# A pinned order for the first chunks of a four-layer decoder trunk, with x loaded in quarters and the second constants loaded later

## The chip, the cores and the metric

The kernel runs on one core of a Trainium2 chip. The metric is device time in microseconds for one execution of the whole program, the lower the better. A profiled execution also gives a trace: the start and length of every instruction on the matrix engine (TensorE, in the rows PE, and PEld for its weight loads), VectorE (DVE), ScalarE (ACT) and GpSimd (POOL), and of the DMA issues on the queue of SyncE (SP) and of ScalarE (ACTq). Times inside an execution count from the start of its span.

## The reference

Four residual layers over x of 256 tokens by 1024 features. Layer i has a token mixer (sliding-window attention with sinks, gated linear attention, forgetting attention, then sliding-window attention again) and a SwiGLU feed-forward part. Ahead of each stands a norm, whose result is shifted and scaled by vectors computed from a conditioning vector c:

```python
c_act = jax.nn.silu(c)
for i in range(DEPTH):
    mod = c_act @ ada_w[i] + ada_b[i]
    sh1, sc1, g1, sh2, sc2, g2 = jnp.split(mod, 6, axis=-1)
    h = rmsnorm(x, norm_gain[i, 0]) * (1 + sc1) + sh1
    x = x + g1 * mixer(h)
    h = rmsnorm(x, norm_gain[i, 1]) * (1 + sc2) + sh2
    x = x + g2 * swiglu(h)
return rmsnorm(x, final_norm)
```

So the very first thing to be computed, before any product of the first mixer, is sh1 and sc1 of layer 0: c times two matrices of 1024 by 1024, which have to come from memory first.

## The kernel before

x is kept on chip feature-major: eight k blocks of 128 features by 256 tokens. Weights are float32 and are streamed once. `Stream` holds a fixed list of items (`items`, L1164), each a transfer of up to 1 MB into one of five `raw` buffers (`load_raw`, L179). An item is issued on the SP queue as soon as, in the order of the list, a buffer is free; SP waits in order, so a load whose buffer isn't free holds up those behind it. A weight item ("w") is split by ACT and DVE into a high part `wh` (a cast, L194) and a low part `wl` (a subtraction, L196), in two pieces; a product of two such split operands is three matmuls (`mm3`, L275 to 279). An "ada" item holds a piece of a matrix that c is multiplied by.

For the first two vectors of layer 0, called here s (the scale, vector 1) and h (the shift, vector 0), an item holds 256 columns, and `ada_rows` (L217) makes 16 small matmuls with c (L228), a copy of the row by ACT (L229), and then a "turn": two small products, four matmul records, that stand the row up into columns (L233), and an addition of the bias on DVE (L235). The list begins, in the letters of `ORDER0`, with s h w s h s h w s h w w w: four pairs of s and h, and between them the weights w0 and w1 of the mixer's first two chunks (`i0_0` keys, `i0_1` values); w2 is the third chunk, `i0_2`.

`first_chunks` (L712) makes the first norm's statistics (squares of the eight k blocks on ACT L422, sums on DVE L433, small matmuls L326, L339, L349, a square root L342), and then goes through four rounds r. A round takes the s and h items of two k blocks, computes their columns of mod and A (`mod_cols`, L378), makes the two k blocks of the normed and shifted input, `hh` and `hl` (`h_tiles`: tk on DVE L452, hh on ACT L454, hl on DVE L447), and multiplies them with w0, and from round 2 on also with w1. (In the rows, hh is the tile of that name; "the h row" is the shift.) The order in which this is written is not the order in which it runs: the tile scheduler sorts each engine's instructions by its own estimate, apart from those marked to keep their place.

The constants come in two transfers: `const` on the SP queue at the beginning, and `const2` (0.67 MB: rotary tables, masks, and the sinks) on ACT's queue within `first_chunks`. `swa` (L751) follows: rotary products of the keys, the products of four more chunks, and the attention. `nsink` (L690) negates the sinks on DVE.

Of the kernel before, what the change touches and what calls it, by code (L numbers as in the profile page):

```python
# [13 lines left out]
AF = mybir.ActivationFunctionType  # L14
ALU = mybir.AluOpType
PSUM = bass.MemoryType.PSUM

P = 128
D = 1024
KT = D // P  # L20
S = 256
# [11 lines left out]
CONST_COLS = [  # L33
    ("ident", 128), ("ones", 2), ("eps", 1), ("gain", DEPTH * 2 * KT), ("ada_b", DEPTH * 48),
    ("fin", KT), ("hnorm", 2), ("bgate", GH), ("bf", 1), ("one", 1), ("c", KT),
]
CONST2_COLS = [
    ("cos", NB * HD), ("sin", NB * HD), ("swamask", 3 * P), ("foxmask", 3 * P), ("scan", S),
    ("sinks", 2 * 16),
]  # L40


# [100 lines left out]
class Builder:  # L143
# [542 lines left out]
    def swa_heads(self, layer, pool, q_of, kT, v, oh, ol):  # L686
# [7 lines left out]
        def head(h):  # L694
            g, i = divmod(h, 4)
            rows = slice((i % 2) * HD, (i % 2 + 1) * HD)

            def pre():
                q = q_of(g)
                if g not in qTs and q is not None:  # L700
                    qTs[g] = self.swa_qT(pool, q)
                return q is not None
            return {
                "pre": pre, "ready": lambda: True,
                "q": lambda: qTs[g][rows, i // 2],
                "k": lambda: kT[0][rows, g],
                "v": lambda: [v[:, b, g * HD:(g + 1) * HD] for b in range(NB)],
                "sink": nsink[:, h:h + 1],
            }
        return self.attn_heads(pool, [head(h) for h in range(16)], self.c("swamask"), oh, ol)  # L710

    def first_chunks(self):  # L712

        nc = self.nc
        self.A, self.late = None, []
        self.st.cap = self.st.widx[EARLY]
        self.per_tick = 0.0
        self.turns = []
        for k in range(KT):
            self.x_done(k, nc.vector)  # L720
        self.stat_start(self.acc)
        self.stat_end()
        self.tc.keep_in_program_order(nc.scalar.dma_start(self.const2, self.a["const2"]))
        rbs = self.t(self.small, [P, S], "rbs", bufs=1)
        nc.scalar.copy(rbs, self.spread(self.y))
        hs = hh, hl = self.h_alloc()
        A = self.t(self.small, [P, KT], "A", bufs=2)
        sh = self.mod[0][:, :KT]
        outs, ws, todo = [], [], []
        for r in range(4):  # L730
            self.st.force_ada(0, (0, 1), r)
            while self.turns:
                self.turns.pop(0)()
            self.mod_cols(0, 0, 2 * r, 2 * r + 2, A)
            self.h_tiles(range(2 * r, 2 * r + 2), rbs, A, sh, hh, hl)
            if r in (0, 2):
                c = len(ws)
                ws.append([x.rearrange("p (k n) -> p k n", k=KT) for x in self.st.get(f"i0_{c}")])
                self.st.cap = self.st.widx[EARLY]
                outs.append(self.banks(("mm", "s")[c])[0])  # L740
                todo.append(0)
            for c, (wh, wl) in enumerate(ws):
                for k in range(todo[c], 2 * r + 2):
                    for m in range(2):
                        sl = slice(m * P, (m + 1) * P)
                        self.mm3(outs[c][m][:, :S], hh[:, k, sl], hl[:, k, sl], wh[:, k], wl[:, k],
                                 k == 0, k == KT - 1)
                todo[c] = 2 * r + 2
        return hs, [[o[:, :S] for o in out] for out in outs]

    def swa(self, layer, oh, ol, pool):  # L751
# [480 lines left out]
    def build(self):  # L1232
        nc, tc, ctx = self.nc, self.tc, self.ctx
        pool = lambda n: ctx.enter_context(tc.tile_pool(name=n, bufs=1))
        cp = pool("const")
        self.wpool = pool("w")
        self.hpool = pool("h")
        self.small = pool("small")
        self.psum = ctx.enter_context(tc.tile_pool(name="ps", bufs=1, space=PSUM))

        self.x = self.t(cp, [P, KT, S], "x")
        self.const = self.t(cp, [P, CONST_W], "const")
        self.const2 = self.t(cp, [P, CONST2_W], "const2")
        self.cact = self.t(cp, [P, D], "cact")
        self.mod = [self.t(cp, [P, 48], f"mod{l}") for l in range(DEPTH)]
        self.gla_wg = self.t(cp, [16, GH * P], "gla_wg")
        self.gla_masks = self.t(cp, [P, 7, P], "gla_masks", U8)

        crow = self.t(self.hpool, [P, KT, S], "hh", bufs=1).rearrange("p k n -> p (k n)")[:1, :D]
        nc.sync.dma_start(crow, self.a["c"])  # L1250
        nc.sync.dma_start(self.const, self.a["const"])
        nc.sync.dma_start(self.x, self.a["x"])
        self.ccol = self.t(self.small, [P, KT, 32], "ccol", bufs=1)
        nc.vector.memset(self.ccol, 0.0)
        nc.scalar.activation(self.ccol[:, :, 0:1], self.c("c").unsqueeze(2), AF.Silu)
        self.st = Stream(self, self.items())
        self.st.issue()
        one = self.t(self.small, [P, S], "fc", bufs=2)[:1, :P]
        nc.vector.memset(one, 1.0)
        for i in range(2):  # L1260
            ps = self.ps("t")
            sl = slice(i * 512, (i + 1) * 512)
            nc.tensor.matmul(ps, one, crow[:, sl], start=True, stop=True)
            nc.scalar.activation(self.cact[:, sl], ps, AF.Silu)

        mixers = [self.swa, self.gla, self.fox]
        for l in range(DEPTH):
            with tc.tile_pool(name=f"mix{l}", bufs=1, reuse_waits="tile") as mp:
                self.layer = l
                self.done_k = 0  # L1270
                oh = self.t(mp, [P, KT, S], "oh", F32R)
                ol = self.t(mp, [P, KT, S], "ol", F32R)
                self.cuts, self.on_pool = CUTS[0], MIX_POOL[l]
                mixers[l % 3](l, oh, ol, mp)
                self.cuts, self.on_pool = CUTS[1], OUT_POOL
                self.out_proj(l, oh, ol, self.mod[l][:, 2 * KT:3 * KT])
            self.cuts, self.on_pool = CUTS[2], FFN_POOL
            self.ffn(l)
        self.final_tile(KT - 1)
        stat = self.ps("o")  # L1280
        self.stat = [stat[:, b:b + 1] for b in range(NB)]
        self.stat_end(self.acc)
        for i, ps in enumerate(self.final):
            o = self.t(self.wpool, [P, WIDE], "raw", bufs=RAW)[:, :512]
            b, half = divmod(i, 2)
            y = self.y[:, b:b + 1]
            if b:
                nc.scalar.activation(o, ps, AF.Copy, scale=y)
            else:
                nc.vector.tensor_scalar(out=o, in0=ps, scalar1=y, scalar2=None, op0=ALU.mult)  # L1290
            (nc.scalar if b else nc.sync).dma_start(
                self.out[b * P:(b + 1) * P, half * 512:(half + 1) * 512], o)
# [108 lines left out]
```

## Time and profile before

| | before |
|---|---|
| median of 3 runs | 1260.54 us (1259.45 to 1266.03) |
| the profiled execution | 1260.51 us |
| its span | 1258.7 us |
| mean granted TensorE clock | 0.986 |
| busy: PE, DVE, ACT, POOL | 96%, 79%, 55%, 11% |
| read from memory | 296.16 MB, 236 GB/s over the span |
| issue of c, const and x on SP | 0.75, 1.15 and 1.56 us |
| first product with c | 14.50 us |
| first product of w2, behind the first chunks | 55.44 us |

A row of the timeline gives the start, the length, the engine, the line, the operation with its output and inputs, and the count of like instructions merged into it; in square brackets stands the idle time of the engine before it and what ended it. Matmul rows are pipelined: the distance between two starts says more than the length of one. The chain of waits follows the last instruction back to what released it, and gives shares of the span.

### The profile page before, as it was taken

What the parts mean: (1) busy time and instruction counts of PE and PEld (TensorE: products, weight loads), DVE (VectorE), ACT (ScalarE), POOL (GpSimd) and SP (SyncE); (2) the same over time, 40 slices, a digit from 0 to 9 for tenths busy, and PEclk for the clock granted to TensorE, in tenths of its full rate; (3) what the DMA queues carried; (4) which work ended last, traced back from release to release, by engine and by line L of the source; (5) the groups of instructions that cost most, each with busy time, mean ns of one, the idle gap of its engine ahead of it and who ended that gap; (6) DMA issues with size and microseconds to landing.
All of it is one profiled execution on the core that took longest, in us unless ns stands there. A gap on an engine that the chain in (4) does not pass through costs nothing.

```text
span 1258.7 us, 19761 instructions
## 1 busy us (share of the span) xinstructions
PE 1207.7 (96%) x7444; PEld 1053.3 (84%) x7444; DVE 1000.2 (79%) x1826; ACT 698.3 (55%) x1294; POOL 136.3 (11%) x177
## 2 busy tenths in 40 slices
PE   5898799999998999999999999999999999999997
PEld 3786788888888998888889999888888979888886
DVE  2598998888779989988878758988888998766553
ACT  3475564444486756444557867544445677544442
POOL 0011110001104412000011101100011011000011
PEclk8898899999999999999999999999999999999999
DMA  8655779977745445988875543699788444665440
GB/s 358 250 220 203 271 282 364 336 284 260 280 148 183 147 141 204 363 323 306 274 281 214 206 174 135 250 349 339 281 274 281 168 164 168 215 220 211 162 162 34
DMA packets 44673, 298.51 MB, mean 237 GB/s; under 512 B 5169, under 2 KB 5329, under 8 KB 14242
## 3 DMA queue, kind: packets, MB, share of 16 engines
q1 hardware_dynamic: 43778, 295.54, 64.9%
q8 instruction: 58, 0.95, 0.3%
q10 hardware_dynamic: 432, 1.20, 0.2%
q0 software_dynamic: 368, 0.53, 0.1%
q14 instruction: 37, 0.30, 0.1%
HBM read 296.16 MB, written 1.05 MB: 236 GB/s over the span
## 4 chain that ended last, share of the span: by engine, by line
PE 84%; DVE 7%; ACT 4%; issue 2%; DMA 2%; POOL 1%; DVEq 0%; SPq 0%; ACTq 0%; POOLq 0%
PE mm L1133 13%; PE mm L277 12%; PE mm L278 11%; PE mm L279 11%; PE s L278 7%; PE s L277 7%; PE s L279 7%; PE mm L1135 7%; PE s L576 2%; DVE wl L196 2%; PE o L606 2%; DVE raw L213 1%; PE t L1104 1%; PE t L617 1%; ACT wh L194 1%
## 5 line engine op out<-in xcount | busy, mean ns | idle before, releaser
L196 DVE TENSOR_TENSOR wl<-raw,wh 128x1024 fp32r<-128x1024 f32 (+2 forms) x408 | 447.2, 1129 | 88.0 <-ACT wh L194 86.9
L194 ACT CAST wh<-raw 128x1024 fp32r<-128x1024 f32 (+2 forms) x408 | 376.2, 964 | 230.7 <-issue 108.8
L1133 PE MATMUL mm<-a,wh 128*128 128x512 f32 x704 | 247.8, 396 | 0.0
L213 DVE CUSTOM_DVE_ANT_0 raw<-raw,cact,const 128x1024 f32<-128x1024 f32 x176 | 224.1, 1292 | 11.2 <-DMA raw<-in_ada 11.1
L277 PE MATMUL mm<-wh,hh 128*128 128x512 f32 (+1 forms) x560 | 198.8, 356 | 6.1 <-ACT hh L454 5.8
L1135 PE MATMUL mm<-a,wl 128*128 128x256 f32 x704 | 197.6, 281 | 0.0
L278 PE MATMUL mm<-wl,hh 128*128 128x512 f32 (+1 forms) x560 | 194.5, 348 | 0.2 <-DVE wl L196 0.2
L279 PE MATMUL mm<-wh,hl 128*128 128x512 f32 (+1 forms) x560 | 193.5, 347 | 0.0
L1133 PEld LDWEIGHTS mm<-a,wh 128*128 128x128 f32 x704 | 132.2, 188 | 30.4
L277 PE MATMUL s<-wh,hh 128*128 128x512 f32 (+2 forms) x384 | 145.1, 379 | 2.9 <-ACT hh L454 2.9
L278 PE MATMUL s<-wl,hh 128*128 128x512 f32 (+2 forms) x384 | 143.6, 375 | 0.6 <-DVE wl L196 0.6
L279 PE MATMUL s<-wh,hl 128*128 128x512 f32 (+2 forms) x384 | 142.1, 374 | 0.0
L433 POOL TENSOR_TENSOR sq<-sq,sq 128x256 f32<-128x256 f32 x48 | 53.9, 1123 | 758.4 <-ACT sq L422 732.2
L1135 PEld LDWEIGHTS mm<-a,wl 128*128 128x128 f32 x704 | 132.6, 188 | 0.2
L277 PEld LDWEIGHTS mm<-wh,hh 128*128 128x128 f32 x560 | 107.0, 191 | 21.3 <-ACT hh L454 6.2
L278 PEld LDWEIGHTS mm<-wl,hh 128*128 128x128 f32 x560 | 107.1, 192 | 12.8 <-issue 0.7
L279 PEld LDWEIGHTS mm<-wh,hl 128*128 128x128 f32 x560 | 106.9, 192 | 13.0 <-issue 0.2
L514 DVE SCALAR_TENSOR_TENSOR x<-mm,mod,x 128x256 f32<-128x256 f32 x128 | 61.5, 481 | 44.7 <-PE mm L1135 37.5
L277 PEld LDWEIGHTS s<-wh,hh 128*128 128x128 f32 x384 | 72.5, 189 | 15.5 <-ACT hh L454 3.4
L278 PEld LDWEIGHTS s<-wl,hh 128*128 128x128 f32 x384 | 72.8, 190 | 12.6 <-DVE wl L196 0.8
L279 PEld LDWEIGHTS s<-wh,hl 128*128 128x128 f32 x384 | 72.2, 190 | 13.1
L277 PE MATMUL mm<-oh,wh 128*128 128x256 f32 x256 | 74.8, 297 | 8.3 <-DVE x L514 8.2
(218 smaller groups left out, 2007.8 us busy)
## 6 DMA issues: line engine op xcount, KB each, us to landing
raw<-in_ada SPq DMA_DIRECT2D x96, 1024.0 KB, 6.3
raw<-in_gu SPq DMA_DIRECT2D x88, 1024.0 KB, 5.6
raw<-in_down SPq DMA_DIRECT2D x64, 704.0 KB, 4.7
raw<-in_swa_in SPq DMA_DIRECT2D x12, 1024.0 KB, 5.3
raw<-in_gla_in SPq DMA_DIRECT2D x11, 1024.0 KB, 4.9
raw<-in_fox_in SPq DMA_DIRECT2D x11, 1024.0 KB, 6.0
raw<-in_swa_o SPq DMA_DIRECT2D x8, 1024.0 KB, 5.0
raw<-in_gla_o SPq DMA_DIRECT2D x4, 1024.0 KB, 4.8
```

The lines of the kernel that those rows point to most:

```text
L194: nc.scalar.copy(wh[:, sl], raw[:, sl])
L196: eng.tensor_tensor(out=wl[:, sl], in0=raw[:, sl], in1=wh[:, sl].bitcast(F32), op=ALU.subtract)
L213: nc.vector.tensor_tensor_reduce(out=w, in0=w, in1=self.cact, scale=1.0, scalar=b, op0=ALU.mult, op1=ALU.add, accum_out=col)
L277: nc.tensor.matmul(out, ah, bh, start=first, stop=False)
L278: nc.tensor.matmul(out, ah, bl, start=False, stop=False)
L279: nc.tensor.matmul(out, al, bh, start=False, stop=last)
L433: (eng or nc.gpsimd).tensor_tensor(out=q, in0=self.acc, in1=q, op=ALU.add)
L514: self.nc.vector.scalar_tensor_tensor(out=self.x[:, m], in0=ps, scalar=gate[:, m:m + 1], in1=self.x[:, m], op0=ALU.mult, op1=ALU.add)
L576: nc.tensor.matmul(sc[:, so:s1], q[:, so:so + P], k[:, :k1], start=True, stop=True)
L606: nc.tensor.matmul(o[rows, b * P:S], vs[e][b], pt[:, e, :S] if b == 0 else pt[:, e, S:], start=b == 0, stop=b == 1)
L1133: nc.tensor.matmul(o, wh[:, k], a[:, kk].rearrange("p e n -> p (e n)"), start=kk == 0, stop=False)
L1135: nc.tensor.matmul(o[:, S:], wl[:, k], a[:, kk, 0], start=False, stop=kk == FT - 1)
```

## The change

- The sinks move from `const2` to `const`.
- x is loaded in four transfers of two k blocks, and the weight stream's first loads are issued before the other preparations.
- Silu of c is computed on the row `crow` before it is spread over the partitions; the two copies to `cact` then run on DVE instead of ACT, out of other banks of PSUM ("mm" instead of "t").
- The squares and sums of the first norm are written out in `first_chunks`.
- In a round, s's product comes first, then chunk 0's products of the round before, then h's product, then both turns and the h tiles. Chunk 1's products all come behind the rounds: first those of six k blocks, then the last two k blocks of both chunks.
- `const2` is issued on ACT's queue at the end of round 1 instead of behind the statistics.
- `pinned` chains all instructions of `first_chunks` on each engine to the order in which they are written.

```diff
 CONST_COLS = [
...
+    ("sinks", 2 * 16),
 ]
 CONST2_COLS = [
...
-    ("sinks", 2 * 16),
 ]
...
+    def pinned(self, start):
+        last = {}
+        for ins in list(self.nc.cur_bb.bb.instructions)[start:]:
+            if ins.engine in last:
+                self.tc.add_manual_dep(
+                    ins, last[ins.engine].name,
+                    mybir.DependencyInfo(mybir.DependencyClass.NoSync, mybir.DependencyReason.DATA),
+                    reason="first chunks")
+            last[ins.engine] = ins
...
     def first_chunks(self):
         nc = self.nc
+        start = len(nc.cur_bb.bb.instructions)
...
+        acc = None
         for k in range(KT):
-            self.x_done(k, nc.vector)
+            q = self.t(self.small, [P, S], "sq", bufs=4)
+            nc.scalar.activation(q, self.x[:, k], AF.Square)
+            if 0 < k < KT - 1:
+                nc.vector.tensor_tensor(out=q, in0=acc, in1=q, op=ALU.add)
+            acc, self.acc = q, acc
+        self.last_sq = acc
         self.stat_start(self.acc)
         self.stat_end()
-        self.tc.keep_in_program_order(nc.scalar.dma_start(self.const2, self.a["const2"]))
...
+        def products(n, chunks=slice(None)):
+            for c, (wh, wl) in list(enumerate(ws))[chunks]:
+                for k in range(todo[c], n):
+                    for m in range(2):
+                        sl = slice(m * P, (m + 1) * P)
+                        self.mm3(outs[c][m][:, :S], hh[:, k, sl], hl[:, k, sl], wh[:, k], wl[:, k],
+                                 k == 0, k == KT - 1)
+                todo[c] = n
         for r in range(4):
-            self.st.force_ada(0, (0, 1), r)
+            self.st.force_ada(0, (1,), r)
+            products(2 * r, slice(1))
+            self.st.force_ada(0, (0,), r)
             while self.turns:
                 self.turns.pop(0)()
             self.mod_cols(0, 0, 2 * r, 2 * r + 2, A)
...
-            for c, (wh, wl) in enumerate(ws):
-                for k in range(todo[c], 2 * r + 2):
...
-                todo[c] = 2 * r + 2
+            if r == 1:
+                nc.scalar.dma_start(self.const2, self.a["const2"])
+        products(KT - 2)
+        products(KT)
+        self.pinned(start)
...
-        nc.sync.dma_start(self.x, self.a["x"])
+        for i in range(4):
+            nc.sync.dma_start(self.x[:, 2 * i:2 * i + 2], self.a["x"][:, 2 * i:2 * i + 2])
+        self.st = Stream(self, self.items())
+        self.st.issue()
         self.ccol = self.t(self.small, [P, KT, 32], "ccol", bufs=1)
         nc.vector.memset(self.ccol, 0.0)
-        nc.scalar.activation(self.ccol[:, :, 0:1], self.c("c").unsqueeze(2), AF.Silu)
-        self.st = Stream(self, self.items())
-        self.st.issue()
         one = self.t(self.small, [P, S], "fc", bufs=2)[:1, :P]
         nc.vector.memset(one, 1.0)
+        nc.scalar.activation(crow, crow, AF.Silu)
+        nc.scalar.activation(self.ccol[:, :, 0:1], self.c("c").unsqueeze(2), AF.Silu)
         for i in range(2):
-            ps = self.ps("t")
+            ps = self.ps("mm")
             sl = slice(i * 512, (i + 1) * 512)
             nc.tensor.matmul(ps, one, crow[:, sl], start=True, stop=True)
-            nc.scalar.activation(self.cact[:, sl], ps, AF.Silu)
+            nc.vector.tensor_copy(self.cact[:, sl], ps)
```

More of the change, by code (lines that the diff above doesn't have):

```diff
@@ L741, in first_chunks @@
                 todo.append(0)
-            for c, (wh, wl) in enumerate(ws):
-                for k in range(todo[c], 2 * r + 2):
[L744 to L747, printed above, removed]
-                todo[c] = 2 * r + 2
+            if r == 1:
[3 more added lines that the diff above has]
+        self.pinned(start)
         return hs, [[o[:, :S] for o in out] for out in outs]
```

## The prediction

> **What bounds the kernel now.** I read the page first, then the begin of the chain of waits, then the timeline of the first 70 us and a table of stages cut at the rounds of `first_chunks`. The page says that the kernel as a whole is TensorE's:
>
> ```profile
> span 1258.7 us, 19761 instructions
> PE 1207.7 (96%) x7444; PEld 1053.3 (84%) x7444; DVE 1000.2 (79%) x1826; ACT 698.3 (55%) x1294; POOL 136.3 (11%) x177
> ...
> PE 84%; DVE 7%; ACT 4%; issue 2%; DMA 2%; POOL 1%; DVEq 0%; SPq 0%; ACTq 0%; POOLq 0%
> ```
>
> The profiled execution took 1260.51 us, 1.81 more than its span; the median of the runs is 1260.54, so a microsecond off the span is taken as one off the median. PE is idle for 1258.7 − 1207.7 = 51 us, and the change can only work on the part that lies in the beginning. There the stages are short and serial (columns: stretch, length, PE, PEld, DVE, ACT and POOL busy with counts, granted clock, DMA share, GB/s):
>
> ```profile
> core 0: us, PE busy (x) PEld busy (x) DVE busy (x) ACT busy (x) POOL busy (x), PEclk, DMA share, GB/s
> 14.50:22.25 7.75, 4.67 (x42) 2.43 (x41) 1.55 (x7) 2.62 (x6) 1.02 (x4) 0.94 1.01 425
> 22.25:25.67 3.42, 3.23 (x13) 2.71 (x13) 2.86 (x4) 1.28 (x2) 0.00 (x0) 0.50 0.78 328
> 25.67:31.77 6.10, 4.15 (x41) 2.06 (x40) 1.38 (x6) 1.30 (x4) 0.00 (x0) 0.78 0.92 340
> 31.77:34.63 2.86, 2.86 (x13) 2.63 (x13) 0.87 (x2) 0.35 (x1) 0.00 (x0) 0.50 0.90 335
> 34.63:39.99 5.36, 3.40 (x42) 1.91 (x41) 1.39 (x6) 1.30 (x4) 0.00 (x0) 0.97 0.61 216
> 39.99:46.86 6.87, 6.24 (x49) 5.90 (x49) 3.23 (x4) 2.23 (x3) 0.00 (x0) 1.00 0.71 247
> 46.86:50.97 4.11, 3.07 (x41) 1.97 (x40) 1.28 (x6) 1.30 (x4) 0.00 (x0) 1.00 0.73 253
> ```
>
> From 14.5 to 51 us no engine is full: rows of products with c (14.50, 25.67, 34.63, 46.86) alternate with rows of products of h, and in the former PE is idle for up to 3 us while ACT and DVE turn a row of mod into h. In two stretches the clock is 0.50 as well. This is a latency chain, so order decides, not work. The end of the stage is the first product of w2 (`i0_2`, the first ordinary chunk), at 55.44:
>
> ```profile
> 55.44 0.28 PE L277 MATMUL mm<-wh,hh 128*128 128x256 f32 x1
> ```
>
> **The start, up to the first product with c (call its time T0).** Before:
>
> ```profile
> 1.56 0.42 SPq L1252 DMA_DIRECT2D x<-in_x  x1
> 2.28 3.75 PE L1263 MATMUL t<-hh,fc 1*128 1x512 f32 x4 [2.28 <-DMA hh<-in_c]
> 3.77 1.28 ACT L1255 ACT_TABLE_LOAD   x1 [3.77 <-DMA const<-in_const]
> 6.07 0.60 ACT L1264 ACTIVATE cact<-t 128x512 f32<-128x512 f32 x1 [0.31 <-PE t L1263]
> 7.03 3.23 ACT L422 ACTIVATE sq<-x 128x256 f32<-128x256 f32 x8 [0.37 <-DMA x<-in_x]
> 7.79 3.08 DVE L433 TENSOR_TENSOR sq<-sq,sq 128x256 f32<-128x256 f32 x6 [6.52 <-ACT sq L422]
> 10.92 1.01 PE L326 MATMUL t<-const,sq 128*128 128x1 f32 x4 [4.89 <-DVE sq L433]
> 14.50 3.56 PE L228 MATMUL t<-raw,ccol 128*32 128x256 f32 x32
> 18.41 1.05 ACT L194 CAST wh<-raw 128x1024 fp32r<-128x1024 f32 x1
> ```
>
> c is there at 2.28; the table load (1.28) now waits for c alone, then Silu runs over 1024 elements of one partition (the nearest row is the cast of 1024 columns, 1.05) and over ccol: ACT is free at about 4.8 instead of 6.67. x in quarters gives the first squares their data earlier; the last quarter can't land before x did, 7.03, and three more issues of 0.42 can put it at 8.3. Eight squares at 3.23 / 8 = 0.40 then end near 8.1 to 9.1, instead of 10.26. But the two copies to cact move from ACT to DVE (the same shape took ACT 0.60), and the second waits for the matmuls, which start only behind Silu: 4.6 + 3.75 = 8.4. The six sums take 3.1 on DVE (last end before: 10.87). Best, copies and sums interleave: about 9.4. Worst, the tile scheduler puts all sums behind the second copy: 8.4 + 0.6 + 3.1 = 12.1. From the last sum to T0 it was 14.50 − 10.87 = 3.6, and nothing in that chain changes but the const2 issue on ACT, which leaves. T0 is 13.0 at best, 15.7 at worst; I take 14.4, the middle, close to the row's 14.50: **no gain here**.
>
> The transfers themselves aren't slowed, I think:
>
> ```profile
> x<-in_x SPq DMA_DIRECT2D x1, 1024.0 KB, 5.4
> const<-in_const ACTq DMA_DIRECT2D x1, 656.0 KB, 8.0
> const<-in_const SPq DMA_DIRECT2D x1, 205.5 KB, 2.5
> ```
>
> 205.5 KB took 2.5 us and 1 MB took 5.4, all of it under way together, so landing times overlap and quarters shouldn't cost four times 2.5. The Trainium skill, "DMA: Bandwidth & Descriptors", section "Measured (HBM→SBUF, 128 partitions, SWDGE, issued from GpSimd)", asks for batches of at least 1 MiB and so speaks against quarters of x. By the page's fixed 2.0 us for each, an estimate one behind the other is 10.4 us for x; the trace's overlap disagrees.
>
> **Round 0.** Before, DVE stood for const2, because the scheduler had put `nsink` (from `sinks`, which lay in const2) ahead of A:
>
> ```profile
> 17.99 1.18 PE L233 MATMUL t<-const,fc 128*128 128x1 f32 x8
> 20.83 0.18 DVE L690 TENSOR_SCALAR nsink<-const 128x16 f32<-128x16 f32 x1 [1.98 <-DMA const<-in_const]
> 21.96 1.22 DVE L196 TENSOR_TENSOR wl<-raw,wh 128x1024 fp32r<-128x1024 f32 x1
> 23.23 0.80 PE L278 MATMUL mm<-wl,hh 128*128 128x256 f32 x2 [0.19 <-DVE wl L196]
> 25.67 1.94 PE L228 MATMUL t<-raw,ccol 128*32 128x256 f32 x16
> ```
>
> 1.98 us of waiting go, since sinks now lie in const. What is late next is the split of w0. Before, its first cast ran at 18.41 under the wait; pinned, both casts stand behind the two hh on ACT. The turns end at T0 + 4.7 (19.17 − 14.50); mod, A, tk and two hh take 2.0 (worked out from round 2's rows below: 0.30 + 0.16 + 0.48 + 0.91, and the gaps), cast 1.05, wl 1.22: the second product runs at T0 + 9.0 = 23.4, as before (23.23). So that gain is spent on the order of the casts. The products, at clock 0.50, take 25.67 − 23.23 = 2.4 again: 25.8. Here the new order first pays: s1's product already ran in the gap, so only h1's is left, 1.94 at half clock: it ends at 27.7. Before, at 25.67, s1's was just starting, and h1's came behind s1's turn.
>
> **Rounds 1 to 3.** Rows of round 2 before, at full clock:
>
> ```profile
> 36.91 1.07 PE L228 MATMUL t<-raw,ccol 128*32 128x256 f32 x16
> 37.28 0.16 DVE L378 SCALAR_TENSOR_TENSOR A<-mod,const 128x2 f32<-128x2 f32 x1
> 37.48 0.88 DVE L452 SCALAR_TENSOR_TENSOR tk<-rbs,A,x 128x256 f32<-128x256 f32 x2
> 38.52 0.61 PE L233 MATMUL t<-const,fc 128*128 128x1 f32 x4 [0.55 <-ACT fc L229]
> 39.43 0.91 ACT L454 ACTIVATE hh<-tk,mod 128x256 fp32r<-128x256 f32 x2 [0.96 <-DVE mod L235]
> 39.99 0.39 PE L277 MATMUL mm<-wh,hh 128*128 128x256 f32 x1 [0.86 <-ACT hh L454]
> 41.44 0.28 PE L279 MATMUL mm<-wh,hl 128*128 128x256 f32 x1
> 43.05 0.28 PE L279 MATMUL s<-wh,hl 128*128 128x256 f32 x1
> 46.65 0.28 PE L279 MATMUL s<-wh,hl 128*128 128x256 f32 x1
> ```
>
> h's product ends at 37.98, and the first product of the new h runs at 39.99: 2.0. Both turns now stand behind h's product, so A (0.16) and the first tk (0.48), which ran under it, come on the path: 2.65. In that gap the turns end after 1.15 (39.13 − 37.98), and the next round's s product (1.07) fits into the 1.5 left. Then 12 products, 41.56 − 39.99 = 1.6, and the next h product, 1.07. A round is 2.65 + 1.6 + 1.07 = 5.3, where before round 2 began at 34.63 and round 3 at 46.86. h2's product ends at 33.0, h3's at 38.3, the last turns at 39.5. Chunk 1's six k blocks, now put off to here, are 36 matmuls of 0.12 (43.05 to 46.65 is thirty): 43.8. They hide the last hh (38.3 + 2.65 = 41.0); without them PE would stand 1.5. The last 24 take 2.9: 46.7. The sum is 55.44 − 46.7 = **8.7 us**.
>
> **What has to be there in time.** SP issues in order, and w1's load stands ahead of s3's and h3's; it waits for w0's buffer, that is for the second half of the split, T0 + 10.2 = 24.6. 1.05 MB at the 425 GB/s of the first row of stages is 2.5 us; with about 1 us to start, w1, s3 and h3 are in by 33.1, and with const2 (0.67 MB, 1.6, now issued behind round 1's hh on ACT, where the copy of s2's row is all that it holds up for 0.4) by 34.7. s3 is wanted at 34.2 and landed near 30.6; h3 is wanted at 37.2. The cover is 2.5 us; beyond it each us costs one. const2 is first read by the rotary products, behind chunk 0's end near 45: 10 us of cover. w1's casts stand behind round 2's hh, near 36; its split ends near 39.5, when chunk 1 starts, no slack.
>
> Behind this nothing hangs on absolute time: the loads follow the buffers, and DVE's queue is full from 80 to 100, so a shift is handed on.
>
> ```profile
> 80.00:100.00 20.00, 18.93 (x152) 15.82 (x150) 20.00 (x67) 14.35 (x46) 6.87 (x12) 1.00 0.60 222
> 100.00:130.00 30.00, 24.15 (x148) 18.16 (x146) 26.08 (x66) 13.32 (x42) 2.48 (x8) 0.84 0.57 199
> ```
>
> With w2's split (two wl of 1.22) now able to run in DVE's idle time, up to 2.4 more could come off that full stretch. One half-clock window would cost 3.4 x (1 − 0.12 / 0.22) = 1.5, where 0.22 is 2.86 / 13 of the row at 31.77. So the forecast is 1260.5 − 8.7 = **1251.8**, its own range 8.7 − 1.4 − 1.5 = 5.8 to 8.7 + 1.4 + 2.4 = 12.5 of gain: 1248.0 to 1254.7.
>
> **Rivals.**
> 1. *Half the beginning cold.* The clock stays at 0.50 after 27.7. Cost against the forecast: two h products 0.87 each, two s products that no longer fit their gap (0.4 each), 24 products at 0.22 instead of 0.13 (2.2), 60 at 0.22 instead of 0.12 (6.0): 10.7, so the stage ends 2.0 us later than before, **1262.5**. It is slower than before from the point at which over 8.7 / 10.7 = 81% of 27 to 47 us is at half clock. For it: 22.25 to 25.67 and 31.77 to 34.63 show 0.50. Against: both follow long gaps of PE, and in the new order PE has 3.7 of each 5.3 us at work. The whole: 0.05. A middle, half of it cold, gives 8.7 − 5.3 = 3.4, **1257.1**: 0.10. The Trainium skill, "TensorE: Matmul & The Clock Gate", section "What's actually happening", says that the array falls to half after an idle window of about 3.4 us; the stretch of 2.86 at 0.50 at 31.77 is of that size.
> 2. *x's quarters land one behind the other.* Four times 2.5 from 1.56 puts the last at 11.6; two squares, the last sum and 3.6 more make T0 16.9 to 17.0, 2.6 later than taken: a gain of 6.1, **1254.4**. The rows' overlap speaks against it: 0.05. The Trainium skill's page cited for x is the rule that would lead here.
> 3. *The pin changes little.* If the scheduler's order already was nearly this, or another wait (w0's split, w1's load) ends each round as late as before, only const2's 1.98 go: **1258.5**. Against it, the rows at 25.67 and 36.91 show s, turn, h, turn and only then the products. 0.12.
> 4. *What lies behind is sorted worse.* The pin ends with `first_chunks`, and the scheduler sorts the rest anew. From 80 to 130 PE is idle 1.07 + 5.85 = 6.9; if that grew by twice as much again, 13.8 − 8.7 = 5.1 slower, **1265.6**; it decides from 8.7 lost on. 0.06.
>
> **How the numbers follow.** Forecast 0.62, rivals 0.05 + 0.10, 0.05, 0.12, 0.06. 0.5% is 6.3 us, about what a measurement of this kernel tells from no change. Faster by more: the forecast, 0.62. Within: the cold cases, the late x and the weak pin, 0.32. Slower by more: rival 4, whose price reaches 6.3 only at its worst, counted whole, 0.06. The range runs from the best of the forecast's own, 1248.0, to past rival 3, 1259.0; outside lie the whole of rival 1, rival 4, and the tails.
>
> **What would show it.** T0 between 13 and 15.7; no DVE wait on const2; second product of round 0 near 23.4; h products ending near 27.7, 33.0 and 38.3; the clock at 1.00 from about 28; 60 matmuls in a row from 39.5; w2's first product near 46.7; and the later stages at the same lengths, each some 8.7 us earlier. I am wrong if PE waits for s3's or h3's load, if the rounds stay above 7 us, or if the lead is gone by 130 us.

## The result, and the profile after

The median of 14 runs of the changed kernel is 1254.2 us (1251.11 to 1257.54), of 14 runs of the kernel before 1264.12 (1259.45 to 1272.07). The ratio is 0.9921, with a 95% interval of 0.9906 to 0.9936: 10 us faster. The profiled execution took 1254.5 us, against 1260.51 before. So trace against trace 6.0 us are gone, and run against run 9.9. The two numbers differ because 1260.5, from which the prediction counted, lies near the lower end of what the kernel before does; its runs and their clock are taken up again at the end of "Why the prediction was right".

The page of the changed kernel, the lines that answer to those shown of before (span and count; busy time of each engine; shares of the chain of waits):

```profile
span 1252.7 us, 19770 instructions
PE 1207.5 (96%) x7444; PEld 1051.5 (84%) x7444; DVE 1001.1 (80%) x1828; ACT 697.8 (56%) x1293; POOL 133.9 (11%) x177
...
PE 85%; DVE 8%; ACT 3%; issue 2%; POOL 1%; DMA 1%; SPq 0%; DVEq 0%; ACTq 0%; POOLq 0%
```

PE is busy for the same time (1207.5 against 1207.7) and idle for 45 us instead of 51. PE's work is the same; what went is waiting. In its timeline the steps that the prediction named (`...` stands for rows left out):

```profile
0.74 1.28 ACT L1287 ACT_TABLE_LOAD   x1 [0.74 <-PEq L1419]
...
3.81 0.17 DVE L690 TENSOR_SCALAR nsink<-const 128x16 f32<-128x16 f32 x1 [2.54 <-DMA const<-in_const]
...
8.68 0.72 ACT L735 ACTIVATE sq<-x 128x256 f32<-128x256 f32 x2 [0.42 <-DMA x<-in_x]
...
10.27 1.02 PE L326 MATMUL t<-const,sq 128*128 128x1 f32 x4 [3.07 <-DVE sq L737]
...
13.84 3.64 PE L228 MATMUL t<-raw,ccol 128*32 128x256 f32 x32
...
18.66 1.07 PE L228 MATMUL t<-raw,ccol 128*32 128x256 f32 x16
...
22.77 0.58 PE L278 MATMUL mm<-wl,hh 128*128 128x256 f32 x1 [0.68 <-DVE wl L196]
...
25.42 1.94 PE L228 MATMUL t<-raw,ccol 128*32 128x256 f32 x16
...
29.08 1.93 PE L228 MATMUL t<-raw,ccol 128*32 128x256 f32 x16
...
33.81 1.66 PE L228 MATMUL t<-raw,ccol 128*32 128x256 f32 x16
...
36.56 1.07 PE L228 MATMUL t<-raw,ccol 128*32 128x256 f32 x16
...
39.98 1.07 PE L228 MATMUL t<-raw,ccol 128*32 128x256 f32 x16
...
49.34 0.28 PE L277 MATMUL mm<-wh,hh 128*128 128x256 f32 x1
```

`nsink` runs at 3.81, as soon as const is there, and holds up nothing. The last squares wait for x's last quarter and start at 8.68. The rows of L228 are, in this order, s0 with h0 (the products with the first items of s and h), s1, h1, s2, h2, s3 and h3. From s1 on each stands alone, where before, in rounds 1 and 2, s, its turn and h followed one another. The last row is w2's first product: 49.34, where it was 55.44. The same table of stages as for the kernel before, cut at this kernel's rounds (stretch, length, PE, PEld, DVE, ACT and POOL busy, clock, DMA share, GB/s):

```profile
13.84:21.51 7.67, 5.89 (x57) 3.04 (x56) 2.17 (x8) 3.01 (x7) 0.00 (x0) 0.99 1.01 427
21.51:25.42 3.91, 3.23 (x13) 2.71 (x13) 2.34 (x2) 1.17 (x2) 0.00 (x0) 0.50 0.95 358
25.42:30.95 5.53, 5.53 (x42) 2.98 (x41) 1.63 (x6) 1.27 (x3) 0.00 (x0) 0.50 0.95 388
30.95:33.81 2.86, 2.86 (x17) 2.64 (x13) 0.52 (x2) 0.38 (x2) 0.00 (x0) 0.50 0.96 369
33.81:38.08 4.27, 3.80 (x41) 2.06 (x41) 1.29 (x6) 0.93 (x3) 0.00 (x0) 0.85 0.97 391
38.08:42.06 3.98, 3.95 (x36) 2.95 (x37) 3.33 (x5) 3.39 (x6) 0.00 (x0) 1.00 0.56 232
42.06:49.34 7.28, 7.28 (x63) 7.28 (x62) 5.78 (x13) 3.52 (x6) 0.00 (x0) 1.00 0.89 348
```

Before, PE was idle in the stretches of products with c for 1.0 to 3.1 us each; here it is full from 25.42 on, but for half a microsecond in the row of 33.81. What is left to see is the clock: 0.50 from 21.5 to 33.8 and still 0.85 in the row behind. The forecast had 1.00 from 28. And the DMA engines (the wire, below) are busier: a share of 0.95 and more up to 38, where the stretch at 34.63 of the kernel before had 0.61.

A clock of 0.50 is called cold below, 1.00 warm. In the traces' records of the clock, cold stretches last 3.41 us or a multiple of it (but for the one in which a trace ends), and one such length is called a window. The changed kernel has four cold windows ahead of w2, from 21.4 to 35.1. The kernel before has four as well: three in its rounds, and one behind the last row that the prediction shows, in the last products ahead of w2. The next row of that table is:

```profile
50.97:55.44 4.47, 4.47 (x25) 4.47 (x25) 3.60 (x10) 2.62 (x5) 0.00 (x0) 0.62 0.81 326
```

So the lead of 6.1 us at w2 was reached with as much cold time as before, 13.7 us in each trace behind its first record of the clock, at about 18: between these two traces, a shorter cold time doesn't explain it.

### The profile page after: what moved, and what is told of

Same layout as the page of the kernel before. It is cut to its first block, busy times and chain, and to the rows that moved or that the text cites. A ratio compares the mean times of both kernels' runs of the same rounds, so it can differ in the third digit from the quotient of the medians.

```text
span 1252.7 us, 19770 instructions
## 1 busy us (share of the span) xinstructions
PE 1207.5 (96%) x7444; PEld 1051.5 (84%) x7444; DVE 1001.1 (80%) x1828; ACT 697.8 (56%) x1293; POOL 133.9 (11%) x177
## 4 chain that ended last, share of the span: by engine, by line
PE 85%; DVE 8%; ACT 3%; issue 2%; POOL 1%; DMA 1%; SPq 0%; DVEq 0%; ACTq 0%; POOLq 0%
PE mm L1160 13%; PE mm L277 12%; PE mm L278 12%; PE mm L279 11%; PE s L277 7%; PE s L278 7%; PE s L279 7%; PE mm L1162 7%; PE s L576 2%; DVE wl L196 2%; PE o L606 2%; DVE raw L213 2%; PE t L1131 1%; ACT wh L194 1%; PE t L617 1%
## 5 line engine op out<-in xcount | busy, mean ns | idle before, releaser
L213 DVE CUSTOM_DVE_ANT_0 raw<-raw,cact,const 128x1024 f32<-128x1024 f32 x176 | 224.2, 1292 | 16.7 <-DMA raw<-in_ada 16.5
L514 DVE SCALAR_TENSOR_TENSOR x<-mm,mod,x 128x256 f32<-128x256 f32 x128 | 61.5, 481 | 42.9 <-PE mm L1162 35.2
```

Of the source, the lines that this page charges most:

```text
L213: nc.vector.tensor_tensor_reduce(out=w, in0=w, in1=self.cact, scale=1.0, scalar=b, op0=ALU.mult, op1=ALU.add, accum_out=col)
L514: self.nc.vector.scalar_tensor_tensor(out=self.x[:, m], in0=ps, scalar=gate[:, m:m + 1], in1=self.x[:, m], op0=ALU.mult, op1=ALU.add)
```

## The experiments

Ratios are to the kernel before, with the 95% interval. "w2" is w2's first product in the profiled execution: 55.44 before, 49.34 in the changed kernel. The theory was that the new order of the rounds is the gain; the rivals were that it was const2, x, the pin as such, or the clock.

**1. The old order, pinned.** The changed kernel, but its rounds in the old order:

```diff
-            self.st.force_ada(0, (1,), r)
-            products(2 * r, slice(1))
-            self.st.force_ada(0, (0,), r)
+            self.st.force_ada(0, (0, 1), r)
...
+            products(2 * r + 2)
             if r == 1:
                 nc.scalar.dma_start(self.const2, self.a["const2"])
-        products(KT - 2)
-        products(KT)
```

> The changed kernel with one part undone: each round is written, and pinned, in the old order (s, h, both turns, h tiles, then the round's products of both chunks); the start, the sinks, x in quarters, const2 after round 1 and the pin stay. My theory (the new order of the rounds is the gain): h1's product can only start behind s1's, near 27, chunk 1's products stand ahead of s3's, and the last products end near 54: w2's first product at 53 to 57 us, within 0.3% of the kernel before (ratio 0.996 to 1.001). Rival (the pin, the constants or x pay): w2's first product near 49.3 as in the changed kernel, ratio near 0.992.

Measured: ratio 0.9976 (0.9959 to 0.9994), w2 at 56.94. Its rounds, in its timeline:

```profile
25.96 3.22 PE L228 MATMUL t<-raw,ccol 128*32 128x256 f32 x32
...
34.74 2.25 PE L228 MATMUL t<-raw,ccol 128*32 128x256 f32 x32
...
46.58 1.93 PE L228 MATMUL t<-raw,ccol 128*32 128x256 f32 x32
...
56.94 0.28 PE L277 MATMUL mm<-wh,hh 128*128 128x256 f32 x1
```

The rounds are 8.8 and 11.8 apart, where those of the kernel before were 9.0 and 12.2 (25.67, 34.63, 46.86). With the start, the constants and the pin all in place the lead is gone from the trace, and of the time 0.24% is left of 0.79%. The order is what pays most, as the theory had it. The clock doesn't explain the difference: the mean granted clock of these runs is 0.987, that of the changed kernel's 0.988.

**2. The new order, not pinned.** The line `self.pinned(start)` is left out.

> The changed kernel without the pin: the text is in the new order, but the scheduler sorts each engine by its own estimate. As it sorts it, h's turn stands apart from s's, chunk 0's products lie partly around the s product, and const2's transfer is the first instruction on ACT, ahead of x on the wire. My theory: the part of the order that the scheduler keeps pays in part, and const2 (0.66 MB at some 425 GB/s) makes x, s0 and h0 up to 1.5 us later: T0 near 15, w2's first product at 50.5 to 54, ratio 0.994 to 0.999. Rival (the pin is not needed, the new text alone does it): w2's first product within 0.7 of 49.3, ratio 0.991 to 0.993.

Measured: ratio 0.9991 (0.9970 to 1.0012), w2 at 53.70:

```profile
0.74 0.38 ACTq L772 DMA_DIRECT2D const<-in_const  x1
...
12.46 1.01 PE L326 MATMUL t<-const,sq 128*128 128x1 f32 x4 [5.05 <-DVE sq L737]
...
16.03 0.66 PE L228 MATMUL t<-raw,ccol 128*32 128x256 f32 x4
```

The scheduler makes const2's transfer ACT's first instruction, and x, const and the statistics come later: 12.46 instead of 10.27, T0 16.03. Its rounds, too, have the turns pulled apart again, and the timed gain is nil. So the text alone does nothing that can be measured: the order pays, and here the pin is what holds it. How much of the loss is the early const2 and how much the order of the rounds, this run does not separate.

**3. The sinks alone.** The kernel before with the entry `("sinks", 2 * 16)` moved from `CONST2_COLS` to `CONST_COLS`, nothing else.

> The kernel before with one part of the change alone: the sinks lie in const, so nsink on DVE does not wait for const2. PE's order is that of the kernel before. My theory: the 1.98 us of DVE's wait go, the second product of round 0 comes at 21 to 22 instead of 23.23, w2's first product 1 to 2 us earlier than 55.4: ratio 0.998 to 0.9995. Rival 3 of the prediction turned round (const2 was most of it): ratio 0.995 or less.

Measured: ratio 0.9981 (0.9964 to 0.9999), in the range expected. But its trace has w2 at 51.21, 4.2 us earlier, and not the 1 to 2 expected. The second product of round 0 (20.93) explains 2.3 of them. The rest goes with the clock, which is cold in one window of the rounds, not three. The lead is then lost. The out projection of layer 0, from the first to the ninth sum into x (L514), in this kernel, the one before and the changed one:

```profile
107.19:139.79 32.60, 24.62 (x143) 19.52 (x141) 26.32 (x57) 13.66 (x34) 0.61 (x4) 0.76 0.57 209
```
```profile
111.45:139.36 27.91, 19.68 (x139) 16.41 (x137) 26.33 (x58) 12.98 (x33) 0.61 (x4) 0.94 0.66 243
```
```profile
105.32:133.21 27.89, 18.63 (x139) 15.36 (x137) 26.31 (x57) 12.96 (x33) 0.60 (x4) 0.95 0.66 244
```

32.60 us at a mean clock of 0.76, against 27.91 at 0.94 and 27.89 at 0.95. What a beginning gains, a cold stretch later can take; it is the same work in all three. That a shift of the beginning made this stretch cold was not tested: it is one trace.

**4. x in one transfer.** The changed kernel with `nc.sync.dma_start(self.x, self.a["x"])`.

> The changed kernel with x in one transfer again; its order on PE behind that is the same. My theory: squares start near 7.0 instead of 5.49 and the last sum is 0 to 0.7 us later, T0 13.8 to 14.5, and what that costs is lost in the noise: ratio to the kernel before 0.991 to 0.994, w2's first product 49.3 to 50.2. Rival (the quarters bring the start forward, and the start counts in full): T0 15 or later, ratio 0.0015 worse than the changed kernel. Rival of the page on DMA (quarters cost): T0 earlier than 13.5.

Measured: ratio 0.9906 (0.9878 to 0.9934), not to be told from the changed kernel's. In the trace the start is later:

```profile
8.41 0.68 DVE L1292 COPY cact<-mm 128x512 f32<-128x512 f32 x1
...
10.40 0.68 DVE L1292 COPY cact<-mm 128x512 f32<-128x512 f32 x1
...
11.01 0.94 DVE L737 TENSOR_TENSOR sq<-sq,sq 128x256 f32<-128x256 f32 x2
```

The squares begin at 7.32, and both copies to cact stand ahead of the last two sums, so T0 is 15.57, 1.7 behind the changed kernel's 13.84; w2 is at 51.10, 0.9 later than the theory had it. The rival was right on T0 (15 or later), but the times don't show that it counts; the other rival, T0 earlier than 13.5, did not happen.

**5 and 6. Both kernels again**, unchanged, for second traces.

> The kernel before, unchanged, for a second trace of it. The runs of before spread from 1257 to 1272 us and the trace that the prediction used (1260.5) lies near their lower end. My theory: the beginning repeats (w2's first product at 55 to 56 us), and what differs lies between 95 and 145 us, in stretches in which the granted clock is 0.50: the first 64 sums into x then end at another time by up to 5 us. Rival: the beginning itself varies, and w2's first product comes up to 4 us later than 55.4.

> The changed kernel, unchanged, for a second trace on the chip of the next two and a ratio beside theirs. My theory: w2's first product at 46 to 50 us, depending on how many of the windows from 21 to 35 us run at clock 0.50 (the first trace: all four, 49.3); ratio 0.990 to 0.994. Rival (the four cold windows were an accident): w2's first product near the forecast 46.7.

Measured: the kernel before took 1261.65 us with w2 at 54.08; the changed kernel's ratio is 0.9925 (0.9899 to 0.9951), with w2 at 49.47.

```profile
54.08 0.28 PE L277 MATMUL mm<-wh,hh 128*128 128x256 f32 x1
```
```profile
49.47 0.28 PE L277 MATMUL mm<-wh,hh 128*128 128x256 f32 x1
```

For the kernel before, both the theory (55 to 56) and its rival (up to 4 us later) missed: w2 came 1.4 us earlier, with one cold window fewer ahead of it, three instead of four, and the later stages did not vary by the 5 us expected. For the changed kernel the theory held: w2 is in its range, and the same four windows are cold.

**7. Split and A earlier.** Round 0's first half of w0's split stands ahead of hh and hl, and A and the first tk ahead of h's part of mod:

```diff
-            while self.turns:
-                self.turns.pop(0)()
+            self.turns.pop(0)()
             self.mod_cols(0, 0, 2 * r, 2 * r + 2, A)
-            self.h_tiles(range(2 * r, 2 * r + 2), rbs, A, sh, hh, hl)
+            tks = []
+            for k in range(2 * r, 2 * r + 2):
+                tk = self.t(self.small, [P, S], "tk", bufs=3)
+                nc.vector.scalar_tensor_tensor(out=tk, in0=rbs, scalar=A[:, k:k + 1], in1=self.x[:, k],
+                                               op0=ALU.mult, op1=ALU.mult)
+                tks.append((k, tk))
+                if self.turns:
+                    self.turns.pop(0)()
+            if r == 0:
+                self.st.piece()
+            for k, tk in tks:
+                nc.scalar.activation(hh[:, k], tk, AF.Identity, bias=sh[:, k:k + 1])
+            for k, tk in tks:
+                nc.vector.scalar_tensor_tensor(out=hl[:, k], in0=tk, scalar=sh[:, k:k + 1],
+                                               in1=hh[:, k].bitcast(F32), op0=ALU.add, op1=ALU.subtract)
```

> The changed kernel with two steps of a round moved on ACT and DVE: the first half of w0's split stands ahead of round 0's hh and hl, and in all rounds A and the first tk stand ahead of h's part of mod. PE's order and all behind the first chunks stay. Theory (PE waits on that split and on A and tk): the second product of round 0 at 21.2 to 21.6 instead of 22.77, and 0.4 to 0.6 off each of four rounds: w2's first product 2.5 to 3.5 us earlier than the changed kernel's on the same clock, and ratio 0.002 to 0.003 better. Rival (the loads or the clock set the rounds, not these): w2's first product within 1 us of it.

Measured: ratio 0.9914 (0.9889 to 0.9939), w2 at 46.22.

```profile
19.88 1.61 PE L228 MATMUL t<-raw,ccol 128*32 128x256 f32 x16 [1.27 <-DMA raw<-in_ada]
...
21.80 0.42 PE L278 MATMUL mm<-wl,hh 128*128 128x256 f32 x1
...
32.73 1.07 PE L228 MATMUL t<-raw,ccol 128*32 128x256 f32 x16 [1.30 <-DMA raw<-in_ada]
...
46.22 0.28 PE L277 MATMUL mm<-wh,hh 128*128 128x256 f32 x1
```

The second product runs at 21.80 instead of 22.77, less than expected, because PE now waits for s1's load (1.27) and later for s3's (1.30): what is late next are the loads. w2 is 3.1 earlier, but on a warmer clock (two cold windows, not four), so not all of it is the split's. The time missed: 0.0007 better than the changed kernel's 0.9921, where 0.002 to 0.003 was expected, and not to be told from it.

**8. Unread products in PE's gap.** In the changed kernel, behind s1's product:

```diff
             self.st.force_ada(0, (1,), r)
+            if r == 1:
+                fill = self.ps("o")
+                for _ in range(5):
+                    nc.tensor.matmul(fill[:, :P], self.c("ident"), self.c("ident"), start=True, stop=True)
             products(2 * r, slice(1))
```

> The changed kernel with five products of ident with ident added on PE, into an unused bank, in the gap ahead of round 0's products (19.7 to 21.5 us); they are read by nobody. Theory (the gap makes the windows from 21.4 on cold): at most two of the four windows from 21 to 35 us are at 0.50, and w2's first product comes 1.5 to 4 us earlier, 45.5 to 48. Rival (cold for another reason, such as products that fill a part of the array only): the four windows stay at 0.50, w2's first product 49 to 50, ratio as the changed kernel's.

Measured: ratio 0.9922 (0.9892 to 0.9951); in the trace w2 at 45.96 and no stretch at 0.50 between 19 and 94 us. Its rounds, cut at the rows of L228 for s1, h1, h2 and h3:

```profile
19.46:25.09 5.63, 4.28 (x40) 3.17 (x39) 4.36 (x8) 3.06 (x5) 0.00 (x0) 1.00 0.93 393
25.09:30.66 5.57, 5.09 (x53) 3.42 (x52) 2.15 (x7) 1.62 (x4) 0.00 (x0) 1.00 0.84 331
30.66:36.61 5.95, 5.18 (x53) 3.46 (x53) 3.11 (x8) 3.20 (x6) 0.00 (x0) 1.00 1.01 424
36.61:45.96 9.35, 9.35 (x84) 8.73 (x85) 7.37 (x16) 4.64 (x8) 0.00 (x0) 1.00 1.01 421
```
```profile
36.61 1.07 PE L228 MATMUL t<-raw,ccol 128*32 128x256 f32 x16 [0.29 <-DMA raw<-in_ada]
```

This is the forecast's beginning on the forecast's clock: rounds of 5.57 and 5.95 (5.3 forecast), 9.35 from h3 to w2 (9.5), w2 at 45.96 (46.7). But h3's product waits 0.29 us for its load, which the forecast did not have. As a trace it confirms the theory; as a time it is the changed kernel's, so that the fill makes the beginning warm as a rule is not shown.

**9. const2 early.** The changed kernel with const2 issued behind the statistics again.

> The changed kernel with const2 issued where it was before, on ACT behind the statistics, 0.64 MB among s1, h1 and s2; PE's order is the changed kernel's everywhere. The trace of the changed kernel and its second trace show s1's product start at 18.66 and, waiting for its load, at 19.67. Theory (the first loads have no slack left): s1 comes 0.7 to 1.6 us later, near 20.5 to 21.3, but the split of w0 ends at 22.8 anyway, so w2's first product is 0 to 0.5 us later on the same clock; ratio 0.991 to 0.995. Rival (const2's late place is a part of the gain): s2 or h2 is waited for too, w2's first product over 1 us later, ratio 0.001 to 0.002 worse.

Measured: ratio 0.9926 (0.9907 to 0.9944), w2 at 45.48.

```profile
20.87 1.94 PE L228 MATMUL t<-raw,ccol 128*32 128x256 f32 x16 [2.14 <-DMA raw<-in_ada]
...
45.48 0.28 PE L277 MATMUL mm<-wh,hh 128*128 128x256 f32 x1
```
```profile
24.97:30.55 5.58, 5.10 (x54) 3.43 (x53) 2.16 (x7) 1.53 (x4) 0.00 (x0) 1.00 1.00 417
```

s1 comes at 20.87 behind 2.14 us of waiting for its load, as expected, and nothing is lost by it in the end. The later const2 is no measurable part of the gain. This trace, with PE's order that of the changed kernel, was cold only from 20.7 to 24.1, and its w2 is 3.9 ahead of the changed kernel's traces: the clock, not the order, makes that difference, and it needs no fill.

**10. Chunk 1 not put off.** `products(2 * r, slice(1))` becomes `products(2 * r)`.

> The changed kernel with chunk 1's products not put off: each round's s product is followed by the last round's products of both chunks, so 36 products of chunk 1 stand between s3's and h3's product. Theory (they delay h3 by 36 x 0.12 = 4.3 us, and then nothing covers the last hh): w2's first product 1.5 to 3 us later than the changed kernel's on the same clock (for a beginning with four cold windows, 51 to 52.5); ratio 0.993 to 0.995. Rival (36 products cost the same wherever they stand): within 0.7 us, ratio as the changed kernel's.

Measured: ratio 0.9954 (0.9938 to 0.9969), w2 at 52.80:

```profile
45.27 1.07 PE L228 MATMUL t<-raw,ccol 128*32 128x256 f32 x16
```

h3's product runs at 45.27 instead of 39.98, behind the 36. w2 is 0.3 later than the theory's range, in a trace that was cold earlier as well (s1's 16 products take 1.93, not 1.07), and the ratio 0.0004 above its range, with an interval that reaches into it. It is 0.0033 worse than the changed kernel's, 4 us. Putting off chunk 1 is thus worth about two fifths of the whole gain (0.0079), and three fifths of what experiment 1 leaves to the order (0.0055).

**11. Split and fill together**, the fill with four products ahead of s1's product.

> Both of the earlier steps together, early half split with A and tk ahead of h's part, and four unread products of ident on PE ahead of s1's product, where PE waits for s1's load. Theory (split and clock are separate costs): no window before 45 us at 0.50, w2's first product at 43.5 to 45, about 1.5 us ahead of either alone; ratio 0.988 to 0.991. Rival (s1's load is now what ends round 0, and the cold windows return for another reason): 45.5 to 46.5, ratio as the early split's, 0.9914.

Measured: ratio 0.9891 (0.9873 to 0.9909), the lowest of all, beside 0.9921 (0.9906 to 0.9936) of the changed kernel; the intervals just overlap. The trace is of its longest run:

```profile
34.26 1.93 PE L228 MATMUL t<-raw,ccol 128*32 128x256 f32 x16 [2.27 <-DMA raw<-in_ada]
...
48.67 0.28 PE L277 MATMUL mm<-wh,hh 128*128 128x256 f32 x1
```
```profile
32.00:36.00 4.00, 1.74 (x16) 0.68 (x16) 3.37 (x7) 2.79 (x4) 0.00 (x0) 0.61 1.01 421
```

PE waited 2.27 us for s3's load, in a stretch where the wire is full (1.01) and PE busy for 1.74 of 4; from 32.9 to 39.7 the clock was 0.50, and w2 came at 48.67. The fill itself held things up: it ran from 19.46 to 21.51 (L761), and s1's product came only at 21.44, though its load, issued at 5.18, had landed 14.3 us later, at 19.5. The theory's trace failed, and the rival's too (45.5 to 46.5); the theory's time held.

**12. const2 after round 2**, in the kernel of 11 (`r == 2` for `r == 1`).

> The kernel of the run before (early half split, A and tk first, four unread products) with const2's transfer issued after round 2 instead of after round 1. In that run PE waited 2.27 us for s3's load, and the granted clock then fell to 0.50 from 32.9 to 39.7. Theory (the wire is full, so const2's 0.64 MB ahead of s3 and h3 cost their 1.5 us): the wait for s3's load falls to 0.3 to 1.2, no cold window after 24 us, w2's first product at 43.5 to 46; ratio 0.986 to 0.990. Rival (s3's load is late because SP issues it behind w1's, which waits for w0's buffer): the wait stays at 2 us or more, w2's first product as before, 48 to 49, ratio 0.989.

Measured: ratio 0.9898 (0.9871 to 0.9926), w2 at 46.76.

```profile
32.23 1.93 PE L228 MATMUL t<-raw,ccol 128*32 128x256 f32 x16 [2.04 <-DVE hl L780]
...
46.76 0.28 PE L277 MATMUL mm<-wh,hh 128*128 128x256 f32 x1
```

The wait ahead of s3's product stays at 2.04, and two cold windows stay too. The row puts the wait down to hl, with which that product shares nothing and which ended at the same time. The load settles it: issued at 23.37, it landed 8.7 us later, at 32.1, just ahead of the product. In experiment 11 it took 10.4 from its issue, so it did come sooner by about the 1.5 that the theory asked; but h2's product ran 1.8 us earlier as well (27.98, there 29.77), so PE waited nearly as long. The rival had the wait right, and s3's issue right behind w1's (22.95); w2 (48 to 49) it had wrong. The ratio is in the theory's range and no better than experiment 11's.

## Why the prediction was right

Forecast 1251.8 from 1260.5, a ratio of 0.9931; measured 0.9921. The direction and the mechanism held: in the new order PE hardly waits in the rounds, and experiment 1 shows that the order makes the difference. That the ratio came so near is in part luck. Trace against trace, which is what the forecast added up, 6.0 of 8.7 us came; the timed gain is larger for a reason that is not in the sum (the last paragraph). By its steps:

- **The start.** T0 forecast 14.4 (13.0 to 15.7), measured 13.84 and, in the second trace, 14.20: right. Copies and sums interleave, as in the best case. Two terms were off, to opposite sides: the table load did not wait for c (0.74), so the product for cact began at 3.42, not 4.6; and x's last quarter, put between 7.03 and 8.3, was there only at 8.68 and 9.70. The quarters were not paid one behind the other, which would have put the last at 11.6, so rival 2 did not happen (its T0 of 16.9 to 17.0 is 16.5 by its own terms). The Trainium skill, "DMA: Bandwidth & Descriptors", section "Measured (HBM→SBUF, 128 partitions, SWDGE, issued from GpSimd)", asks for transfers of at least 1 MiB. This case agrees in direction: x in one transfer (experiment 4) was there at 7.32, 1.4 us ahead of the last quarter. But its first squares came 1.8 us later than those of the first quarter (5.49), and so did its T0, by 1.7.
- **const2.** The wait of 1.98 went, as forecast, and was spent on the split of w0, as forecast: second product forecast 23.4, measured 22.77 and 22.99. Experiment 3 shows it alone, 0.2% of time. There it came 6.3 us behind T0 (20.93 from 14.60), in the changed kernel 8.9: that much the pinned order of this stage gave away.
- **Round 1.** h1's product forecast to end at 27.7; it ended at 27.36.
- **Rounds 2 and 3.** "The clock at 1.00 from about 28" failed: 0.50 to 35 in both traces of the changed kernel. h2's product ended at 35.47 instead of 33.0, h3's at 41.05 instead of 38.3. This is the term that was off in the traces, by 49.34 − 46.7 = 2.6 us. It is rival 1 in part: 7.4 us behind 27.7 were cold, and a quarter of its price of 10.7 was paid. What the prediction held against it, that cold stretches follow long gaps of PE, does not hold: in the kernel before, the one at 31.77 followed 0.86 us of idle time, and here PE had none from 25.42 to 33.81 and stayed cold. On a warm clock (experiments 8 and 9) a round is 5.6 us, once 5.95, against 5.3 summed, and w2 is at 45.5 to 46.0. The 0.3 lies in a round's 12 products, which take 1.9 (38.08 to 39.98), not 1.6.
- **The last 24 products.** The sum has them at 2.9, on a warm clock, and they ran warm. In the kernel before they had not (the row at 50.97 above), so some of the 8.7 was a warmer clock, and the prediction doesn't name it.
- **Chunk 1 behind the rounds.** Forecast to hide 1.5 of the last hh; undone it cost 4 us, because its 36 products then stand ahead of h3's. The forecast's path already had h3 free of them, so its total is not touched; only this step by itself was priced too low.
- **The loads.** s3 and h3 were never waited for in the changed kernel, but the cover was thinner than 2.5, and in part it was the cold rounds that gave it. The loads took longer than it had them: w1's 5.8 us from its issue at 23.88, not 3.5 (of which 1 us to start stands without a row), and s3's came at 32.2 (issued at 24.30, 7.9 to landing), not near 30.6. On the forecast's own clock (8) h3 waited 0.29 for its load, one of the prediction's signs of being wrong, and where round 2 was another 1 to 1.5 us earlier (7, 11), s3 waited 1.30 and 2.27.
- **Handed on.** The lead is 6.1 at w2, 6.0 at the end of the span, and 6.1 and 6.1 at the two cuts of the out projection (111.45 − 105.32, 139.36 − 133.21). Rival 4 did not happen here; the 2.4 of w2's split did not come on top. Experiment 3 shows a loss like it, through the clock.
- **The weak pin** (1258.5, a ratio of 0.9984) was wrong for the change as made, and near the mark for its text alone: without the pin the ratio is 0.9991, and with the old order pinned 0.9976.

Why 9.9 us by times are 6.0 by traces: the kernel before gave 1260.5 and 1261.7 in its traces, while the medians of its runs lay at 1262.6 to 1264.6; the changed kernel gave 1254.5 and 1255.6, at or above its medians of 1254.2 and 1252.4. The mean granted clock of each run shows a part of the reason. It is 0.983 on average over the 64 runs of the kernel before beside the experiments, 0.986 and 0.987 in its two traces, and 0.988 over the 20 runs of the changed kernel, 0.987 and 0.988 in its traces. So the kernel before was traced in executions warmer than most of its own, and the timed runs are warmer in the new order. Among the 64, the 34 with a clock of 0.983 or less took 1265.4 us on average, the other 30 1262.1. What makes the runs of the new order warmer, and whether the clock accounts for all of the 3.9 us, stays open.

## What to carry to other kernels

In a serial beginning, count for each engine what stands queued between one round's result and the next round's first input, and put work that is ready into that gap; a scheduler that sorts by its own estimate may undo it, so the order has to be held. Work that nobody waits for (here chunk 1) belongs behind the chain, not inside it. And once such a chain is short, look at the loads and at the granted clock before shortening it further. Compare traces at the same amount of cold time: two traces of one kernel differed by 1.4 us at w2 with one window more or less (experiment 5).

## What the runs showed of the hardware that was not expected

- **The clock column says 1.00 where it has no record.** The changed kernel's first products with c take 3.64 us for 32 (13.84), 0.11 each; sixteen at 36.56 take 1.07, 0.067 each. The column says 0.99 for the stretch from 13.84, but the trace's records of the clock begin at 18.0. There the distance between like matmuls tells the clock, not the column.
- **A busy PE may stay cold.** From 25.42 to 33.81 PE had no idle time in the rows, and the clock was 0.50; in experiment 8 the stretch from 25.09 to 30.66 ran at 1.00 with 0.48 us idle. The Trainium skill, "TensorE: Matmul & The Clock Gate", section "What's actually happening", releases the clock after one busy window of some 3.4 us. Here 8.4 us of rows without a gap didn't. In experiment 9 the same rows, from 24.97 to 30.55, ran at 1.00 after the clock had come back at 24.1, so the rows alone do not decide it. The products with c use 32 of 128 columns (128*32 in the rows), and the turns' products one column, which may be a part of why; no run tests it.
- **The wire is full at the beginning.** Its busy share is 0.95 and more from 13.84 to 38.08, at 358 to 427 GB/s, and where the rounds were faster (7, 8, 11) PE waited for loads: what these rounds can still give lies in the loads and, by 3.9 us at w2 in experiment 9, in the clock.
